# A fused two-block kernel: where the SSD's decayed inputs are made, and how row norms reach all partitions

## The chip, the cores and the metric

The kernel runs on one core of a Trainium2 chip. A core has TensorE (PE: matmuls; PEld: its weight loads), VectorE (DVE), ScalarE (ACT), GpSimd (POOL) and SyncE (SP, which here issues nearly all DMA transfers), an on-chip memory of 128 partitions (SBUF), matmul accumulators (PSUM) and DRAM. The metric is the device time of one execution in microseconds (us), lower is better, as the median of several runs.

## The reference

The input x is 512 tokens by 1024 channels, float32. The first block prepends 16 meta tokens and computes one projection of the normalised input, from which come

- an SSD (state space) branch: a causal convolution of 3072 channels; dt = softplus; per head cs = cumsum(dt * a) over a chunk; the inputs x * dt; a term inside the chunk, `y_diag = (C B^T * exp(cs_l - cs_s)) (x dt)`; a state per chunk, `states = B^T (exp(cs_end - cs) * x dt)`, carried along the chunks; then y * silu(z), **an RMS norm over each of 4 groups of 512 channels**, and a projection to 1024 channels;
- a sliding-window attention branch with meta tokens and sinks;
- gates for both, an output projection and the residual, then a convolutional feed-forward with its own RMS norm.

The second block normalises again and computes an HGRN2 recurrence and a latent attention (**RMS norms of the query and key-value latents**), gates, an output projection, the residual and a last RMS norm. An RMS norm is `y = x * rsqrt(mean(x*x) + eps)` over the channels, one factor per token.

## The kernel before

Activations lie channels on partitions and tokens along the free dimension: eight tiles of 128 channels by 528 tokens in the first block (514 where the 14 earliest tokens are no longer needed), 128 by 512 in the second. Each float32 operand of the large matmuls is split into a high and a low part, and three matmuls (L88, L89, L90) make one product. A weight tile of 128 by 1024 is loaded by SP (`wload`, L71, two buffers `wraw`), split by ACT (`whi`, L76) and by DVE (`wlo`, L77), three buffers each, and used for two halves of the tokens. PSUM tiles have tags with a number of buffers: in the first block ps_g (the projections) 3, ps_a 2, ps_t 2, ps_o 1.

Since channels are on partitions, the factor of a norm is a row of tokens that every partition needs. `SumSq` adds squares, `sums` (L169) sums them over the partitions by matmuls with a column of ones, which leaves one value per token with tokens on partitions (103 partitions by 5 columns for 514 tokens, 128 by 4 for 512). `rsqrt` computes the factor there with small DVE instructions (rq_m, rq_u, rq_y; L107 to L112, three Newton steps). `bcast_rows` then turns it back: for every column of rq_y one fp32 matmul against the identity (L129), in which rq_y is broadcast as the weight, puts the row on all 128 partitions of a PSUM tile, and ACT copies it to SBUF (L131), with a factor if wanted. `norm512` is the same for 128 by 4.

The SSD runs over four groups of eight heads, in chunks of 106 tokens. `group_tiles` makes the convolved B, C and four x tiles (xs) of the next group, `pair_a` and `pair_b` handle two heads at a time: `pair_a` transposes xs by PE (L384, a PSUM tile for chunks 0 to 3, another for chunk 4), DVE multiplies by dt into xd (L385), GpSimd multiplies xd of chunks 0 to 3 by the decay to the chunk's end into xe (L390), and xe with the transposed B gives the chunk states (L409). E, the decay inside a chunk, starts as a DMA that broadcasts one row of the cumulative sums in DRAM (csd) to all partitions (L397) and is finished by GpSimd and ACT; L440 multiplies it with xd. `pair_b` makes the gate z, adds the parts of y and splits the result into yh and yl.

After the last pair of a group, `group_end` computes the group's factor rq_y, broadcasts it into Rg (with the factor 0.5 that the gate's form needs) and returns four `branch` jobs. A branch job loads a weight tile, runs four gemms of twelve matmuls (two output tiles, two halves of the tokens) into ps_g, and DVE multiplies each by Rg into acc or bt (L477), which frees the PSUM tile. The jobs of a group are handed out among the pairs of the next group; those of the last group run beside the attention. In the second block R1 (the factor of the second block's input, used in `block_input`, L874) and the factors of the kv and q latents (`norm` in `lora_jobs`, tiles with tag lf) go through `norm512`.

No order is written out by hand beyond the program's text. A planner (`TileContext` with `schedule_with_timeline_sim=True`) simulates the program with its own costs, takes for every engine and queue the ready instruction that stands first in the text (weight loads are marked as of high priority), and fixes that order; on the chip each engine and each DMA queue works through its list strictly in order and waits on semaphores. Two instructions that share a tile's buffer wait for each other in the same way.

Of the kernel before, what the change touches and what calls it, by code (L numbers as in the profile page):

```python
# [23 lines left out]
NO = 514  # L24
# [106 lines left out]
        nc.scalar.activation(dst[:, c0 * rows:e], ps[:, :e - c0 * rows], AF.Copy, scale=fac)  # L131


class SumSq:


# [34 lines left out]
                    start=(i == 0 and c == 0), stop=(i == m and c == self.nchunk - 1))  # L171
        return ps[:r, :self.nchunk]

    def rstd(self, width, tag, ptag="t"):
        return rsqrt(self.g, self.sums(ptag), self.rows, self.nchunk, 1.0 / width, tag)


def pcol(g, name, i=0, n=1):
# [36 lines left out]
class Mixer:  # L215
# [50 lines left out]
    def steps(self, wk, dp):  # L266
        g, nc = self.g, self.nc
        wd = [t.rearrange("p a b -> p (a b)") for t in self.w0]
        slots = [tuple(t[:, k * 32:k * 32 + 32] for t in wd) for k in range(8)]
        dtf = wk.tile([32, NTP], F32, name="dtf", tag="ec", bufs=2)  # L270
        nc.gpsimd.memset(dtf[:, NT:NTP], 0.0)
        o = 0
        for n in H1:
            ps = psum(g, "a")
            gemm(g, ps[:32, :n], slots, self.u, o, n)
            nc.vector.tensor_tensor(dtf[:, o:o + n], ps[:32, :n], self.R[:32, o:o + n], ALU.mult)
            o += n
        pst = psum(g)
        for c in range(NCH):
            nc.tensor.transpose(pst[:CH, c * 32:c * 32 + 32], dtf[:, c * CH:(c + 1) * CH], g.ident[:32, :32])  # L280
        sm = lambda nm: wk.tile([128, NCH, 32], F32, name=nm, tag=nm, bufs=1)
        dt, cs, dst, dec, da = sm("dt"), sm("cs"), sm("dstt"), sm("dec"), sm("da")
        dtr, au, sz, sp = da, dst, cs, dec
        fl = lambda t: t.rearrange("p a b -> p (a b)")[:CH]
        dtb = g.par[:CH, _BP["dtb"]:_BP["dtb"] + 32].unsqueeze(1).broadcast_to([CH, NCH, 32])
        nc.vector.tensor_tensor(dtr[:CH], pst[:CH, :NCH * 32].rearrange("p (a b) -> p a b", a=NCH), dtb, ALU.add)
        nc.vector.scalar_tensor_tensor(fl(au), fl(dtr), -1.0, fl(dtr), ALU.mult, ALU.max)
        nc.scalar.activation(fl(au), fl(au), AF.Exp, scale=-1.0)

        nc.vector.tensor_scalar(fl(sp), fl(au), 1.0, 2.0, ALU.mult, ALU.add)  # L290
        nc.vector.reciprocal(fl(sp), fl(sp))
        nc.vector.tensor_tensor(fl(au), fl(au), fl(sp), ALU.mult)
        nc.vector.tensor_tensor(fl(sz), fl(au), fl(au), ALU.mult)
        nc.vector.tensor_scalar(fl(sp), fl(sz), 1.0 / 17.0, None, ALU.mult)
        for k in (15, 13, 11, 9, 7, 5, 3):
            nc.vector.scalar_tensor_tensor(fl(sp), fl(sp), 1.0 / k, fl(sz), ALU.add, ALU.mult)
        nc.vector.scalar_tensor_tensor(fl(sp), fl(sp), 1.0, fl(au), ALU.add, ALU.mult)
        nc.vector.tensor_scalar(fl(sp), fl(sp), 2.0, None, ALU.mult)
        nc.vector.scalar_tensor_tensor(fl(sp), fl(dtr), 0.0, fl(sp), ALU.max, ALU.add)
        nc.vector.memset(dt[:], 0.0)  # L300
        nc.vector.tensor_copy(dt[:CH, :NCH - 1, :], sp[:CH, :NCH - 1, :])
        nl = NT - CH * (NCH - 1)
        nc.vector.tensor_copy(dt[:nl, NCH - 1, :], sp[:nl, NCH - 1, :])
        ea = wk.tile([128, 32], F32, name="ea", tag="ea", bufs=1)
        nc.scalar.activation(ea, g.par[:, _BP["alog"]:_BP["alog"] + 32], AF.Exp)
        nc.vector.scalar_tensor_tensor(da[:CH], dt[:CH], -1.0, ea[:CH].unsqueeze(1).broadcast_to([CH, NCH, 32]), ALU.mult, ALU.mult)
        pc = psum(g)
        nc.tensor.matmul(pc[:CH, :NCH * 32], g.tri[:CH, :CH], fl(da), start=True, stop=True)
        pt = psum(g)
        nc.tensor.matmul(pt[:, :NCH * 32], g.ones[:CH, :], fl(da), start=True, stop=True)  # L310
        nc.scalar.activation(fl(cs), pc[:CH, :NCH * 32], AF.Copy)
        decf = dec.rearrange("p a b -> p (a b)")
        nc.vector.tensor_tensor(fl(dst), pt[:CH, :NCH * 32], fl(cs), ALU.subtract)
        nc.scalar.activation(fl(dst), fl(dst), AF.Exp)
        nc.scalar.activation(decf, pt[:, :NCH * 32], AF.Exp)
        cst = wk.tile([32, NTP], F32, name="cst", tag="ec", bufs=2)
        for c0, c1 in ((0, 3), (3, 5)):
            px = psum(g)
            for c in range(c0, c1):
                nc.tensor.matmul(px[:32, (c - c0) * CH:(c - c0 + 1) * CH], da[:CH, c, :], g.tri[:CH, :CH], start=True, stop=True)  # L320
            nc.scalar.activation(cst[:, c0 * CH:c1 * CH], px[:32, :(c1 - c0) * CH], AF.Copy)
        csd = dp.tile([32, NTP], F32, name="csd", tag="csd", bufs=1)
        nc.sync.dma_start(out=csd, in_=cst)
        self.dt, self.cs, self.dst, self.dec, self.csd = dt, cs, dst, dec, csd
# [48 lines left out]
    def pair_a(self, wk, gi, i):  # L373

        g, nc = self.g, self.nc
        cbm, bt, C, xs = self.grp
        dt, cs, dst, dec = self.dt, self.cs, self.dst, self.dec
        h0 = gi * 8 + 2 * i
        xd = wk.tile([128, NCH, 128], F32, name="xd", tag="xd", bufs=2)
        dtx = lambda c0, c1, t: t[:CH, c0:c1, h0:h0 + 2].unsqueeze(3).broadcast_to([CH, c1 - c0, 2, 64])  # L380
        for c0, c1 in ((0, 4), (4, 5)):
            px = psum(g)
            for c in range(c0, c1):
                nc.tensor.transpose(px[:CH, (c - c0) * 128:(c - c0 + 1) * 128], xs[i][:, c * CH:(c + 1) * CH], g.ident)  # L384
            nc.vector.tensor_tensor(  # L385
                xd[:CH, c0:c1, :].rearrange("p c (h d) -> p c h d", h=2),
                px[:CH, :(c1 - c0) * 128].rearrange("p (c h d) -> p c h d", h=2, d=64),
                dtx(c0, c1, dt), ALU.mult)
        xe = wk.tile([128, 4, 128], F32, name="xe", tag="xe", bufs=1)
        nc.gpsimd.tensor_tensor(  # L390
            xe[:CH].rearrange("p c (h d) -> p c h d", h=2),
            xd[:CH, 0:4, :].rearrange("p c (h d) -> p c h d", h=2), dtx(0, 4, dst), ALU.mult)
        Es = []
        ec = wk.tile([128, NTP], F32, name="ec", tag="ec", bufs=2)
        for k in range(2):
            E = wk.tile([128, NTP], F32, name="E", tag="E", bufs=4)
            nc.sync.dma_start(out=E, in_=self.csd[h0 + k:h0 + k + 1, :].broadcast_to([128, NTP]))  # L397
            hk = slice(k * 64, k * 64 + 64)
            nc.scalar.activation(ec[hk, CH:], E[hk, CH:], AF.Exp)
            nc.gpsimd.tensor_tensor(  # L400
                r3(E)[:CH], cs[:CH, :, h0 + k:h0 + k + 1].broadcast_to([CH, NCH, CH]), r3(E)[:CH], ALU.subtract)
            nc.scalar.activation(E[:CH, :], E[:CH, :], AF.Relu)
            nc.scalar.activation(E[:CH, :], E[:CH, :], AF.Exp, scale=-1.0)
            nc.gpsimd.tensor_tensor(E[:CH, :], E[:CH, :], cbm[:CH, :], ALU.mult)
            Es.append(E)

        px = psum(g)
        for c in range(4):
            nc.tensor.matmul(px[:, c * 128:(c + 1) * 128], bt[:CH, c, :], xe[:CH, c, :], start=True, stop=True)  # L409
        S = wk.tile([128, 4, 128], F32, name="S", tag="S", bufs=2)  # L410
        nc.scalar.activation(S[:, 0, :], px[:, 0:128], AF.Copy)
        for c in range(1, 4):
            for k in range(2):
                ks = slice(k * 64, k * 64 + 64)
                nc.vector.scalar_tensor_tensor(
                    S[:, c, ks], S[:, c - 1, ks], dec[:, c, h0 + k:h0 + k + 1],
                    px[:, c * 128 + k * 64:c * 128 + k * 64 + 64], ALU.mult, ALU.add)
        return xd, Es, ec, S, C, xs[i]
# [38 lines left out]
    def group_end(self, wk, gi):  # L457

        g = self.g
        rg = self.ssq.rstd(2048.0, "g", "o")  # L460
        Rg = self.mp.tile([128, NO], F32, name="Rg", tag="Rg", bufs=2)
        bcast_rows(g, Rg, rg, ROWS, 5, NO, 0.5, "o")
        rhs = self.rhs
        return [lambda c2=c2: self.branch(wk, gi, c2, rhs, Rg) for c2 in range(4)]

# [354 lines left out]
class Block2:  # L820
# [191 lines left out]
    def lora_jobs(self):  # L1012
# [42 lines left out]

        def norm(name):
            r = self.t("lf")
            norm512(g, self.rl[name], r)
            self.rl[name] = (self.rl[name], r)

        def gate(h):
# [138 lines left out]
    def run(self, r1, r12):  # L1200
        self.forgets()
        self.R1 = self.t("R1")
        norm512(self.g, r1, self.R1)
        self.ya = []
        jobs, kpe, norm = self.lora_jobs()
        prev = self.hgrn_a(0)
# [138 lines left out]
def two_hybrid_blocks(ctx, tc, aps):  # L1345
# [21 lines left out]
    g.ones = cp.tile([128, 128], F32, name="ones", tag="ones")  # L1367
    nc.gpsimd.memset(g.ones, 1.0)
    h1 = []
    first_mixer(g, h1)  # L1370
    ffn(g, h1)
    pctx.close()
# [155 lines left out]
```

## Time and profile before

| | |
|---|---|
| median of 3 runs | 1819.78 us (1816.46 to 1825.48) |
| the profiled execution | 1816.29 us, its span 1814.5 us |
| PE busy | 1760.9 us (97%) |
| DVE busy | 1135.3 us (63%) |
| ACT busy | 752.0 us (41%) |
| POOL busy | 321.8 us (18%) |
| DMA | 158.34 MB, mean 87 GB/s |
| mean granted TensorE clock | 0.992 |

The profile gives, for one execution, busy times by engine, groups of instructions (source line, engine, operation, tile written <- tiles read, shapes, count | busy us, mean ns of one | idle time of the engine before them, with what ended it), the chain of waits followed back from the last instruction, DMA issues with the time from issue to landing, and a timeline. An fp32 matmul leaves two records. Matmuls overlap, so the mean of one is longer than what it costs in a row of them.

### The profile page before, as it was taken

Reading aid. Unit: us, or ns where it says so; the run is one execution under the profiler, and the core shown is the slowest. Engines: PE = TensorE matmul, PEld = TensorE weight load, DVE = VectorE, ACT = ScalarE, POOL = GpSimd, SP = SyncE. Lnnn points to the kernel's source line nnn. Section 1 sums busy time; section 2 is a strip of 40 time slices with the busy share of each in tenths; the row PEclk is TensorE's granted clock in tenths of the full one; section 3 lists DMA queues with packets and bytes.
Section 4 is the critical chain, followed back from the end, with each engine's and each line's share of the span. In section 5 each row is a group of like instructions: output and inputs, shape, how many; then the busy total and the mean of one; then the engine's idle time right before and its main releaser. Section 6 shows DMA issues by size and latency. Waiting matters only on the chain.

```text
span 1814.5 us, 29816 instructions
## 1 busy us (share of the span) xinstructions
PE 1760.9 (97%) x12068; PEld 1588.9 (88%) x12068; DVE 1135.3 (63%) x2140; ACT 752.0 (41%) x1326; POOL 321.8 (18%) x300
## 2 busy tenths in 40 slices
PE   7999999999899999999999999999999899999997
PEld 7989999999898889999999888878888777788886
DVE  7897787855586645466666533576665467743453
ACT  4444444422345643343444333554342445532332
POOL 2344445523330001200000011100000121000112
PEclk9999999999999999999999999999999999999998
DMA  3323232232222132222222222222222121222222
GB/s 142 106 85 105 82 106 84 94 106 84 100 81 66 63 105 94 94 82 94 91 85 93 90 94 96 82 93 70 70 70 93 54 73 48 70 92 94 93 90 73
DMA packets 51310, 158.34 MB, mean 87 GB/s; under 512 B 5922, under 2 KB 9764, under 8 KB 51172
## 3 DMA queue, kind: packets, MB, share of 16 engines
q1 hardware_dynamic: 49252, 153.91, 25.1%
q10 hardware_dynamic: 1872, 2.39, 0.4%
q8 instruction: 95, 1.56, 0.3%
q14 instruction: 43, 0.35, 0.1%
q0 software_dynamic: 48, 0.13, 0.0%
HBM read 152.93 MB, written 2.16 MB: 85 GB/s over the span
## 4 chain that ended last, share of the span: by engine, by line
PE 84%; DVE 7%; ACT 3%; issue 2%; POOL 2%; DMA 2%; SPq 0%; DVEq 0%; POOLq 0%; ACTq 0%
PE ps_g L88 22%; PE ps_g L90 22%; PE ps_g L89 22%; PE ps_g L810 2%; PE ps_g L809 2%; PE ps_g L811 2%; DVE wlo L77 1%; DVE cv L336 1%; PE ps_o L1194 1%; DMA E<-csd 1%; PE ps_t L642 1%; PE ps_a L953 1%; POOL xe L390 1%; PE ps_a L440 1%; PE ps_t L409 1%
## 5 line engine op out<-in xcount | busy, mean ns | idle before, releaser
L76 ACT ACTIVATE whi<-wraw 128x1024 fp32r<-128x1024 f32 (+2 forms) x265 | 274.7, 1037 | 571.3 <-PE ps_g L89 348.8
L77 DVE TENSOR_TENSOR wlo<-wraw,whi 128x1024 fp32r<-128x1024 f32 (+3 forms) x259 | 335.0, 1294 | 151.7 <-ACT whi L76 151.0
L88 PE MATMUL ps_g<-uh,whi 128*128 128x264 f32 (+2 forms) x1056 | 303.7, 288 | 2.4 <-DVE z L186 1.4
L90 PE MATMUL ps_g<-uh,wlo 128*128 128x264 f32 (+2 forms) x1056 | 300.9, 285 | 0.0
L89 PE MATMUL ps_g<-ul,whi 128*128 128x264 f32 (+2 forms) x1056 | 300.7, 285 | 0.0
L88 PEld LDWEIGHTS ps_g<-uh,whi 128*128 128x128 f32 x1056 | 199.4, 189 | 4.7 <-DVE z L186 1.6
L88 PE MATMUL ps_g<-fh,whi 128*128 128x258 f32 (+1 forms) x704 | 199.9, 284 | 0.8 <-DVE fx L186 0.8
L89 PE MATMUL ps_g<-fl,whi 128*128 128x256 f32 (+1 forms) x704 | 200.3, 285 | 0.0
L90 PE MATMUL ps_g<-fh,wlo 128*128 128x256 f32 (+1 forms) x704 | 199.9, 284 | 0.0
L90 PEld LDWEIGHTS ps_g<-uh,wlo 128*128 128x128 f32 x1056 | 199.2, 189 | 0.7 <-issue 0.5
L89 PEld LDWEIGHTS ps_g<-ul,whi 128*128 128x128 f32 x1056 | 199.1, 189 | 0.3 <-issue 0.2
L88 PE MATMUL ps_g<-vh,whi 128*128 128x512 f32 x464 | 185.6, 400 | 1.8 <-DVE lf L842 1.8
L89 PE MATMUL ps_g<-vl,whi 128*128 128x512 f32 x464 | 184.6, 398 | 0.0
L90 PE MATMUL ps_g<-vh,wlo 128*128 128x512 f32 x464 | 183.9, 396 | 0.3 <-DVE wlo L77 0.3
L159 POOL TENSOR_TENSOR sq<-sq 128x514 f32<-128x514 f32 (+2 forms) x48 | 61.9, 1298 | 499.1 <-ACT sq L151 499.1
L88 PEld LDWEIGHTS ps_g<-fh,whi 128*128 128x128 f32 x704 | 134.0, 190 | 1.0 <-DVE fx L186 1.0
L89 PEld LDWEIGHTS ps_g<-fl,whi 128*128 128x128 f32 x704 | 134.5, 191 | 0.0
L90 PEld LDWEIGHTS ps_g<-fh,wlo 128*128 128x128 f32 x704 | 134.5, 191 | 0.0
L88 PEld LDWEIGHTS ps_g<-vh,whi 128*128 128x128 f32 x464 | 87.4, 188 | 20.4 <-ACT whi L76 2.2
L90 PEld LDWEIGHTS ps_g<-vh,wlo 128*128 128x128 f32 x464 | 87.2, 188 | 19.6 <-DVE wlo L77 0.8
L89 PEld LDWEIGHTS ps_g<-vl,whi 128*128 128x128 f32 x464 | 87.3, 188 | 18.4
L88 PE MATMUL ps_g<-yh,whi 128*128 128x258 f32 (+1 forms) x256 | 75.8, 296 | 1.7 <-DVE bt L477 1.1
(434 smaller groups left out, 3834.8 us busy)
## 6 DMA issues: line engine op xcount, KB each, us to landing
wraw<-in_w_in SPq DMA_DIRECT2D x128, 512.0 KB, 3.2
wraw<-in_w_ffn_in SPq DMA_DIRECT2D x44, 512.0 KB, 3.2
E<-csd SPq DMA_DIRECT2D x32, 265.0 KB, 4.1
wraw<-in_w_ssd SPq DMA_DIRECT2D x16, 512.0 KB, 3.2
wraw<-in_w_out SPq DMA_DIRECT2D x16, 512.0 KB, 3.3
wraw<-in_w_ffn_out SPq DMA_DIRECT2D x16, 512.0 KB, 3.2
wraw<-in_w_pab SPq DMA_DIRECT2D x16, 512.0 KB, 3.3
wraw<-in_w_att SPq DMA_DIRECT2D x8, 512.0 KB, 3.2
```

Of the source, the lines that this page charges most:

```text
L76: nc.scalar.activation(hf[:, :n], raw[:, :n], AF.Copy)
L77: (eng or nc.vector).tensor_tensor(lf[:, :n], raw[:, :n], hf[:, :n].bitcast(F32), ALU.subtract)
L88: nc.tensor.matmul(ps, wh, a, start=(i == 0), stop=False)
L89: nc.tensor.matmul(ps, wh, b, start=False, stop=False)
L90: nc.tensor.matmul(ps, wl, a, start=False, stop=(i == last))
L159: self.g.nc.gpsimd.tensor_tensor(a[:, :self.ntok], a[:, :self.ntok], sq[:, :self.ntok], ALU.add)
L336: nc.vector.scalar_tensor_tensor(cv, xr[:, j:j + NT], w(j), cv, ALU.mult, ALU.add)
L390: nc.gpsimd.tensor_tensor(xe[:CH].rearrange("p c (h d) -> p c h d", h=2), xd[:CH, 0:4, :].rearrange("p c (h d) -> p c h d", h=2), dtx(0, 4 ...
L409: nc.tensor.matmul(px[:, c * 128:(c + 1) * 128], bt[:CH, c, :], xe[:CH, c, :], start=True, stop=True)
L809: nc.tensor.matmul(ps, wh, uh, start=(k == 0), stop=False)
L810: nc.tensor.matmul(ps, wh, ul, start=False, stop=False)
L811: nc.tensor.matmul(ps, wl, uh, start=False, stop=(k == NFF - 1))
```

## The change

1. **Decayed inputs.** In `steps`, the decay factors `dst` are multiplied by dt once (one DVE instruction). In `pair_a`, xe is then made by DVE from the transposed x in PSUM and `dst`, right after the first part of xd; GpSimd's instruction on xd goes away.
2. **Norms by DRAM.** A new function, `bcast_dram`, writes the factor from SBUF into a row in DRAM, in token order, and reads that row back into all 128 partitions, two transfers on SP's queue, the second dependent on the first. It takes the place of the broadcast by matmuls and ACT for the four group norms (103 by 5), for R1 and for the kv and q latents (128 by 4): seven calls. The factor 0.5 of the group norm moves into rsqrt (`fac`). The other norms stay as they were: the first block's input, the feed-forward's, r12 of the second block, the last one.

```diff
+def bcast_dram(g, pool, dst, y, rows, nchunk, ntok):
+
+    nc = g.nc
+    d = pool.tile([1, nchunk * rows], F32, name="rowd", tag="rowd", bufs=2)
+    nc.sync.dma_start(out=d.rearrange("o (c r) -> (o r) c", r=rows), in_=y)
+    nc.sync.dma_start(out=dst, in_=d[:, :ntok].broadcast_to([128, ntok]))
@@ class SumSq
-    def rstd(self, width, tag, ptag="t"):
-        return rsqrt(self.g, self.sums(ptag), self.rows, self.nchunk, 1.0 / width, tag)
+    def rstd(self, width, tag, ptag="t", fac=1.0):
+        f = fac ** -2.0
+        return rsqrt(self.g, self.sums(ptag), self.rows, self.nchunk, f / width, tag, EPS * f)
@@ steps
         nc.scalar.activation(fl(dst), fl(dst), AF.Exp)
+        nc.vector.tensor_tensor(fl(dst), fl(dst), fl(dt), ALU.mult)
@@ pair_a
                 dtx(c0, c1, dt), ALU.mult)
-        xe = wk.tile([128, 4, 128], F32, name="xe", tag="xe", bufs=1)
-        nc.gpsimd.tensor_tensor(
-            xe[:CH].rearrange("p c (h d) -> p c h d", h=2),
-            xd[:CH, 0:4, :].rearrange("p c (h d) -> p c h d", h=2), dtx(0, 4, dst), ALU.mult)
+            if c0 == 0:
+                xe = wk.tile([128, 4, 128], F32, name="xe", tag="xe", bufs=1)
+                nc.vector.tensor_tensor(
+                    xe[:CH].rearrange("p c (h d) -> p c h d", h=2),
+                    px[:CH].rearrange("p (c h d) -> p c h d", h=2, d=64), dtx(0, 4, dst), ALU.mult)
@@ group_end
-        rg = self.ssq.rstd(2048.0, "g", "o")
+        rg = self.ssq.rstd(2048.0, "g", "o", 0.5)
         Rg = self.mp.tile([128, NO], F32, name="Rg", tag="Rg", bufs=2)
-        bcast_rows(g, Rg, rg, ROWS, 5, NO, 0.5, "o")
+        bcast_dram(g, g.dp, Rg, rg, ROWS, 5, NO)
@@ lora_jobs, norm
-            norm512(g, self.rl[name], r)
+            bcast_dram(g, g.dp, r, self.rl[name], 128, 4, NX)
@@ Block2.run
-        norm512(self.g, r1, self.R1)
+        bcast_dram(self.g, self.g.dp, self.R1, r1, 128, 4, NX)
@@ two_hybrid_blocks
+    g.dp = ctx.enter_context(tc.tile_pool(name="rows", bufs=1, space=bass.MemoryType.DRAM))
```

## The prediction

> **What bounds the kernel now.** I read the page first, its shares and its chain of waits.
>
> ```profile
> span 1814.5 us, 29816 instructions
> PE 1760.9 (97%) x12068; PEld 1588.9 (88%) x12068; DVE 1135.3 (63%) x2140; ACT 752.0 (41%) x1326; POOL 321.8 (18%) x300
> PE 84%; DVE 7%; ACT 3%; issue 2%; POOL 2%; DMA 2%; SPq 0%; DVEq 0%; POOLq 0%; ACTq 0%
> ```
>
> PE is busy 97% of the span and carries 84% of the chain, so the kernel is a stream of matmuls. An edit gains what it takes out of that stream or out of the few places where PE stands, and loses wherever it makes PE stand. All of this execution is 1816.29 us, 1.8 us more than its span, and lies 3.5 us under the median of the runs, 1819.78. I add to the execution's time; the offset to the median is a fifth of a percent.
>
> The diff works mostly in the SSD groups, which in the timeline fill 80 to 500 us. The busy times of that stretch:
>
> ```profile
> core 0: us, PE busy (x) PEld busy (x) DVE busy (x) ACT busy (x) POOL busy (x), PEclk, DMA share, GB/s
> 80.00:500.00 420.00, 404.10 (x3503) 395.05 (x3501) 305.92 (x539) 173.18 (x264) 187.29 (x177) 1.00 0.28 93
> ```
>
> PE stands still for 16 us of 420 there; DVE is busy 73% and has room. Now the groups of instructions that the diff removes or relieves (busy, mean, and the engine's idle time before them):
>
> ```profile
> L129 PE MATMUL ps_t<-mats,rq_y 128*128 128x128 f32 (+3 forms) x54 | 7.2, 275 | 0.9 <-DVE rq_y L112 0.9
> L129 PE MATMUL ps_o<-mats,rq_y 103*128 103x103 f32 (+1 forms) x40 | 6.1, 283 | 5.3 <-DVE rq_y L112 4.7 <-ACT Rg L131 0.6
> L409 PE MATMUL ps_t<-xe,bt 106*128 106x128 f32 x128 | 17.8, 282 | 6.4 <-POOL xe L390 6.0 <-POOL xr L330 0.3
> L390 POOL TENSOR_TENSOR xe<-xd,dstt 106x512 f32<-106x512 f32 x16 | 25.1, 1571 | 24.8 <-DVE xd L385 24.8
> ```
>
> Of PE's 16 us, 6.0 go to waits for GpSimd's xe and 5.3 to waits around the broadcasts of the groups' norms. The stage's stalls are thus exactly where the change works.
>
> **The change part by part: xe.** Before, xe follows two steps: DVE writes xd, then GpSimd takes 1571 ns. After, DVE makes it from the same PSUM tile. Its nearest price is the first part of xd, same shape, same source:
>
> ```profile
> L385 DVE TENSOR_TENSOR xd<-ps_t,dt 106x512 f32<-106x512 f32 x16 | 10.9, 680 | 0.0
> ```
>
> xe comes 0.68 us after xd instead of 1.57 or more, so I credit PE with the whole wait of 6.0 us. DVE gets 16 times 0.68 = 10.9 us more, which its idle 114 us of the stretch cover; if none of it were covered this part would lose 4.9 us. The one extra multiplication of the decay factors by dt, a small DVE instruction (160 elements a partition), is put at nothing; its cover is the same DVE idle time.
>
> **Three norms of the second block** (R1, and those of kv and q). Each loses four fp32 matmuls, eight of the 54 records of the first L129 row; 24 of 54 by 7.2 us is 3.2 us off PE. Each gains two transfers on SP's queue. Their rows are complete early: R1's first reader and the attention's weights come later, and I put the transfers at nothing; if the queue holds back the weights and rope copies behind the q norm, a transfer of some 3 to 4 us could show once.
>
> **The norms of the four groups** decide the case. Before: rsqrt on DVE (rq_y), five matmuls into ps_o, two evictions by ACT (Rg), and the DVE products that free the ps_g tiles of the first branch gemms. After: rq_y, a write into DRAM (time w, from the issue to landing), a wait of SP for it, a read back to 128 partitions, the same products. Group 0 in the timeline, first PE, then DVE:
>
> ```profile
> 164.24 1.13 PE L440 MATMUL ps_a<-E,xd 106*64 106x106 f32 x20
> 167.04 1.11 PE L129 MATMUL ps_o<-mats,rq_y 103*128 103x103 f32 x8 [1.67 <-DVE rq_y L112]
> 171.21 0.39 PE L88 MATMUL ps_g<-yh,whi 128*128 128x256 f32 x1
> 165.86 1.03 DVE L112 SCALAR_TENSOR_TENSOR rq_y<-rq_u,rq_y 103x5 f32<-103x5 f32 x1
> 169.16 0.75 DVE L477 TENSOR_TENSOR acc<-ps_g,Rg 128x258 f32<-128x258 f32 x2
> ```
>
> Three quarters of the branch's first unit have already run by 164.2 and hold all three ps_g tiles, so every later projection waits for Rg. The fourth quarter resumes at 171.21. The read back looks like the reads of E, which broadcast one DRAM row of nearly the same length; the write has the store of csd as its nearest row, 32 rows with few, long pieces:
>
> ```profile
> E<-csd SPq DMA_DIRECT2D x32, 265.0 KB, 4.1
> csd<-cst SPq DMA_DIRECT2D x1, 66.2 KB, 2.6
> ```
>
> So the quarter resumes at 166.89 (end of rq_y) + w + 4.1 + 0.4 (the product) = 171.4 + w: a loss of 0.2 + w, with the matmuls' saving already in it. The other groups:
>
> ```profile
> 268.51 0.16 DVE L112 SCALAR_TENSOR_TENSOR rq_y<-rq_u,rq_y 103x5 f32<-103x5 f32 x1
> 273.12 0.36 PE L88 MATMUL ps_g<-yh,whi 128*128 128x256 f32 x1
> 365.48 0.17 DVE L112 SCALAR_TENSOR_TENSOR rq_y<-rq_u,rq_y 103x5 f32<-103x5 f32 x1
> 378.61 0.42 DVE L477 TENSOR_TENSOR bt<-ps_g,Rg 128x258 f32<-128x258 f32 x1
> 381.54 0.37 PE L88 MATMUL ps_g<-yh,whi 128*128 128x256 f32 x1
> 498.48 0.17 DVE L112 SCALAR_TENSOR_TENSOR rq_y<-rq_u,rq_y 103x5 f32<-103x5 f32 x1
> 500.97 0.45 PE L88 MATMUL ps_g<-yh,whi 128*128 128x256 f32 x1
> 360.00:372.00 12.00, 1.40 (x10) 1.29 (x10) 1.00 0.25 87
> ```
>
> Group 1 resumes at 268.67 + w + 4.5 against 273.12: loss 0.1 + w. Group 3: 498.65 + w + 4.5 against 500.97: loss 2.2 + w. Group 2 runs other projections first: Rg is there at 365.65 + w + 4.1, is read at 378.61, and the fourth quarter comes only at 381.54, so w is hidden up to 11.4 us and PE saves 1.4 us (last row: the L129 matmuls' busy time in that window). Together 1.1 + 3w, and beyond 11.4 us another w - 11.4.
>
> What SP holds meanwhile: while it waits for w, the weights and E loads behind it stay unissued.
>
> ```profile
> SPq L71 <- DVE wlo L77: 1192.6, 211, 15.6
> ```
>
> SP already stands 5.7 us on average for a free weight buffer, so the loads run ahead of PE; and during w PE stands for Rg anyway. I add nothing for it.
>
> **What w is.** In each of the 103 partitions five neighbouring values go to DRAM addresses 412 bytes apart, so the row is 515 pieces of 4 bytes. No row shows such a store. From below it is 2.6 us, as if pieces cost nothing or were spread over 16 engines (32 each). From above come the smallest payloads of the trace: a window with one load of 128 pieces of 512 bytes, and one at the end with stores of 1 KB:
>
> ```profile
> DMA  0000010222147265687765644531111100000000
> DMA packets 144, 0.07 MB, mean 82 GB/s; under 512 B 16, under 2 KB 144, under 8 KB 144
> q1 hardware_dynamic: 144, 0.07, 28.4%
> ```
>
> ```profile
> DMA packets 1152, 1.05 MB, mean 300 GB/s; under 512 B 128, under 2 KB 1152, under 8 KB 1152
> q1 hardware_dynamic: 576, 0.52, 43.2%
> q10 hardware_dynamic: 576, 0.52, 42.6%
> ```
>
> The first window is 0.8 us: 28.4% of 16 engines is 3.6 us, 28 ns for each of 128; but the eight pieces of an engine take some 0.5 us (the digits, 0.02 us each), 64 ns apart. The second is 3.5 us: 85.8% of 16 engines over 1024 pieces, 47 ns for 1 KB. A line through 28 and 47 ns leaves 9 ns for a piece of almost nothing. I assume the 515 pieces run one behind the other on one engine (103 has no divisor by which the rows could be dealt out evenly), at 18 ns, the middle between 9 and 28: w = 2.6 + 9.5 = 12.1 us. Ends: 2.6 us, and 2.6 + 515 x 64 ns = 35.6 us.
>
> The Trainium skill speaks to this choice in "DMA: Bandwidth & Descriptors", section "Why a DMA increments its semaphore by 16 and not by 1": a transfer uses the largest number of engines up to 16 that divides the outermost sizes, and 127 rows fall on one engine. By that rule 103 rows use one and the three 128-row norms sixteen; no run here shows it yet. Were the 515 pieces spread instead, the sum would end near the lower bound below.
>
> **The sum.** Groups 1.1 + 36.3 + 0.7 = 38.1; xe -6.0; three norms -3.2: +28.9. 1816.3 + 28.9 is 1845 us, slower by 1.4%. DVE wholly uncovered would add 10.9, the q norm 4.
>
> **Rivals.** *The short write*: w between 2.6 and 7.2 us (9 ns a piece). The sum is 3w - 8.1: -0.3 to +13.5, so 1816 to 1830. For it speaks that stores of 1 KB at the end run without gaps. *The long write*: at 64 ns a piece, w = 35.6: groups 1.1 + 106.8 + 24.2, less 9.2, gives 1939. For it: a 4-byte store is further from a long one than anything in the trace, and the 512-byte pieces did stand 64 ns apart. *The other side*: the planner, which orders every engine by its own estimate of when things are ready, sees the longer way of Rg and puts the branch's first gemms behind other projections in all groups, as they stand in group 2. Then w is hidden up to some 11 us, and PE loses 6.1 + 3.2 us of matmuls, 5.3 of waits around them and 6.0 for xe: 20.6 us, 1796. It decides wherever 12 us of other projections precede the branch. Against it: in groups 0, 1 and 3 the gemms need only the split rows and the weights, not Rg, and nothing in the order before shows that Rg's lateness held them back. *Not what it says*: xe waits as long for DVE as it did for GpSimd, because DVE's queue is ordered otherwise; then 6.0 us are missing, 1851.
>
> **How the numbers follow.** A difference under 0.5%, 9 us, cannot be told from no change in these runs. The forecast (serial pieces of 9 to 28 ns, w to 17 us, 1830 to 1865) gets 0.42, with the missing xe gain 0.03; the short write 0.23, nearly all within 0.5%; the long one 0.17; the hidden one 0.15. Faster 0.15, same 0.22, slower 0.63. The likeliest's own range is 1830 to 1865. The range asked for runs from 1800 to 1905: it leaves out half of the hidden case and half of the long one.
>
> **What would show it.** In the issues of transfers a row for rowd with its time to landing (w, 12 us by me, and 3 to 4 us for the norms of 128 rows); PE standing before an L88 matmul of the branch in groups 0, 1 and 3, ended by a DVE product that waits for the DMA into Rg, w longer than now; no such wait in group 2; no wait for xe before the L409 matmuls, and DVE instructions of some 0.68 us for xe. I am wrong if w is under 5 us, if the branch gemms come behind other projections, or if PE stands for weights instead.

## The result, and the profile after

The changed kernel takes 1869.79 us as the median of 5 runs (1868.17 to 1870.42), beside 1819.78 us (1816.46 to 1825.66) for the kernel before in the same comparison: a ratio of 1.0276, 95% interval 1.0258 to 1.0293. It is slower by 50 us, where 29 were forecast; 1869.8 lies 5 us above the likeliest case's own range of 1830 to 1865, and within the whole range of 1800 to 1905. Its profiled execution took 1868.29 us.

The page of the changed kernel, its span and its engines:

```profile
span 1866.5 us, 29730 instructions
PE 1764.2 (95%) x12004; PEld 1590.6 (85%) x12004; DVE 1136.1 (61%) x2157; ACT 747.6 (40%) x1314; POOL 290.9 (16%) x284
```

PE stands still for 1866.5 - 1764.2 = 102.3 us, against 53.6 us before: 48.7 of the 52 us by which the span grew. The other 3.3 us are PE busy for longer, and that is odd, for the edit took 3.2 + 6.1 = 9.3 us of matmuls away. So the matmuls that stayed took some 12.6 us more than before. Both parts are found below.

The group of the branch's first matmuls (instruction and shape, count | busy, mean of one | PE's idle time just before them and what ended it), first of the kernel before, then of the changed one:

```profile
L88 PE MATMUL ps_g<-yh,whi 128*128 128x258 f32 (+1 forms) x256 | 75.8, 296 | 1.7 <-DVE bt L477 1.1 <-DVE xr L186 0.4
```

```profile
L88 PE MATMUL ps_g<-yh,whi 128*128 128x258 f32 (+1 forms) x256 | 77.6, 303 | 43.8 <-DVE bt L488 31.3
```

Idle time before this one group went from 1.7 to 43.8 us. Group 0 in the timeline (start, duration), SP's queue, then DVE, then PE:

```profile
163.09 0.30 SPq L138 DMA_DIRECT2D rowd<-rq_y  x1
173.65 0.34 SPq L139 DMA_DIRECT2D Rg<-rowd  x1
```

```profile
162.91 0.15 DVE L112 SCALAR_TENSOR_TENSOR rq_y<-rq_u,rq_y 103x5 f32<-103x5 f32 x1
178.80 1.09 DVE L488 TENSOR_TENSOR acc<-ps_g,Rg 128x258 f32<-128x258 f32 x3 [12.15 <-DMA Rg<-rowd]
```

```profile
179.29 0.58 PE L88 MATMUL ps_g<-yh,whi 128*128 128x256 f32 x1 [12.07 <-DVE acc L488]
179.67 0.41 PE L89 MATMUL ps_g<-yl,whi 128*128 128x256 f32 x1
182.83 0.28 PE L89 MATMUL ps_g<-ul,whi 128*128 128x258 f32 x1
```

The store is issued at 163.09 and the read back, which waits for it, at 173.65: w is 10.6 us. The read back is in use 5.15 us later, and PE, which had no free PSUM tile, stood for 12.07 us. The last two rows show something else: matmuls of the same kind last 0.41 us just after the stall and 0.28 us from 182.83 on.

The other groups, end of rq_y on DVE and PE's next branch matmul:

```profile
276.30 0.16 DVE L112 SCALAR_TENSOR_TENSOR rq_y<-rq_u,rq_y 103x5 f32<-103x5 f32 x1
526.68 0.17 DVE L112 SCALAR_TENSOR_TENSOR rq_y<-rq_u,rq_y 103x5 f32<-103x5 f32 x1
```

```profile
292.94 0.58 PE L88 MATMUL ps_g<-yh,whi 128*128 128x256 f32 x1 [10.20 <-DVE bt L488]
543.02 0.58 PE L88 MATMUL ps_g<-yh,whi 128*128 128x256 f32 x1 [13.63 <-DVE bt L488]
```

Group 2 ought to have hidden its row behind other projections. Its SP queue, DVE and PE:

```profile
387.98 0.24 SPq L138 DMA_DIRECT2D rowd<-rq_y  x1
398.62 0.32 SPq L139 DMA_DIRECT2D Rg<-rowd  x1
399.04 0.86 SPq L71 DMA_DIRECT2D wraw<-in_w_in  x2
```

```profile
406.75 1.22 DVE L77 TENSOR_TENSOR wlo<-wraw,whi 128x1024 fp32r<-128x1024 f32 x1 [9.57 <-ACT whi L76]
407.89 1.08 DVE L488 TENSOR_TENSOR bt<-ps_g,Rg 128x258 f32<-128x258 f32 x3
```

```profile
408.36 0.58 PE L88 MATMUL ps_g<-yh,whi 128*128 128x256 f32 x1 [6.34 <-DVE bt L488]
```

Here the product with Rg has no wait of its own. It stands in DVE's queue behind a weight split, the split waits for its weights, and the weights were issued only at 399.04, after SP had been held for 10.6 us. PE stands for 6.34 us on a chain that starts in SP's queue.

In the second block R1 and the q norm cost stalls too, by two different ways; SP first, then DVE at R1, then PE:

```profile
1193.36 0.39 SPq L138 DMA_DIRECT2D rowd<-rq_y  x1
1203.49 0.34 SPq L139 DMA_DIRECT2D R<-rowd  x1
1468.79 0.38 SPq L138 DMA_DIRECT2D rowd<-rq_y  x1
1476.88 0.33 SPq L139 DMA_DIRECT2D lf<-rowd  x1
1477.31 2.51 SPq L1088 DMA_DIRECT2D th<-lf  x4
```

```profile
1207.44 5.39 DVE L885 SCALAR_TENSOR_TENSOR h<-h,par,R 128x512 f32<-128x512 f32 x8 [10.46 <-DMA R<-rowd]
```

```profile
1216.29 0.49 PE L88 MATMUL ps_g<-vh,whi 128*128 128x512 f32 x1 [3.87 <-ACT whi L76]
1486.41 1.25 PE L1017 MATMUL ps_t<-mats,o 128*128 128x128 f32 x4 [7.22 <-ACT o L1013]
```

These stores have 128 rows, and still w is 10.1 and 8.1 us. At R1 the row itself is late: DVE waits 10.46 us for it, ACT works on what DVE makes, the next weight split (whi) stands behind that in ACT's queue, and PE waits for the split. At q the four rope copies (th) are late: SP issues them only at 1477.31, after it was held; DVE's product with them waits 8.53 us, and the factor rq_y of another norm, for which ACT's L1013 waits, stands behind that product. The kv row, whose read back is issued 33 us after its store with five weight loads in between, costs no stall of over 1 us.

### The profile page after: what moved, and what is told of

Its sections match the earlier page's. It is cut to its first block, busy times and chain, and to the rows that moved or that the text cites. A ratio compares the mean times of both kernels' runs of the same rounds, so it can differ in the third digit from the quotient of the medians.

```text
span 1866.5 us, 29730 instructions
## 1 busy us (share of the span) xinstructions
PE 1764.2 (95%) x12004; PEld 1590.6 (85%) x12004; DVE 1136.1 (61%) x2157; ACT 747.6 (40%) x1314; POOL 290.9 (16%) x284
## 3 DMA queue, kind: packets, MB, share of 16 engines
q8 instruction: 94, 1.54, 0.4%
## 4 chain that ended last, share of the span: by engine, by line
PE 63%; DVE 4%; DMA 2%; ACT 1%; issue 1%; SPq 0%; DVEq 0%; ACTq 0%
PE ps_g L88 16%; PE ps_g L90 16%; PE ps_g L89 16%; PE ps_g L821 2%; PE ps_g L820 2%; PE ps_g L822 2%; DMA rowd<-rq_y 2%; PE ps_o L1205 1%; PE ps_a L964 1%; PE ps_t L653 1%; PE ps_o L664 1%; DVE wlo L77 0%; PE ps_a L615 0%; PE ps_o L663 0%; PE ps_o L644 0%
## 5 line engine op out<-in xcount | busy, mean ns | idle before, releaser
L88 PE MATMUL ps_g<-yh,whi 128*128 128x258 f32 (+1 forms) x256 | 77.6, 303 | 43.8 <-DVE bt L488 31.3
```

The source lines that it names most:

```text
L88: nc.tensor.matmul(ps, wh, a, start=(i == 0), stop=False)
```

## The experiments

The edits are shown against the kernel before, unless another is named. `bcast_dram` and `fac` are those of the change.

**One part at a time.** Three kernels each hold one part of the change.

*xe alone.*

```diff
+        nc.vector.tensor_tensor(fl(dst), fl(dst), fl(dt), ALU.mult)
-        xe = ... nc.gpsimd.tensor_tensor(xe, xd[:CH, 0:4, :], dtx(0, 4, dst), ALU.mult)
+            if c0 == 0:
+                xe = ... nc.vector.tensor_tensor(xe, px[:CH], dtx(0, 4, dst), ALU.mult)
```

> The kernel before with part 1 alone: xe by VectorE from PSUM, all norms by matmuls. Theory (the two parts add up, and xe is nearly worthless): the changed kernel still shows 5.9 us of TensorE waits for xe, as the one before did (6.0), so 0 to 3 us faster, 1817 to 1820 us. My prediction's own step: 6.0 us faster, 1814. Rival (VectorE, 10.9 us busier, is what slows the changed kernel): 5 us slower or more.

Measured: 1813.29 us against 1819.24 before, ratio 0.9966 (0.9953 to 0.998): 6.0 us faster, as the prediction's own step had it; the theory that xe is nearly worthless is out. The group that uses xe, in this kernel and then in the changed one:

```profile
L411 PE MATMUL ps_t<-xe,bt 106*128 106x128 f32 x128 | 17.4, 279 | 4.1 <-DVE xe L392 3.9
```

```profile
L420 PE MATMUL ps_t<-xe,bt 106*128 106x128 f32 x128 | 18.0, 284 | 5.9 <-DVE xe L401 5.9
```

The size is the forecast's, but PE still waits 3.9 us for xe, now for DVE's, where it waited 6.0. The rows put some 2 us of the gain at this wait. PE's idle time fell by 3.4 us in all in the profiled execution, which was 4.3 us faster than that of the kernel before; which other waits the rest of the 6.0 came from is not settled.

*The four groups' norms alone.*

```diff
-        bcast_rows(g, Rg, rg, ROWS, 5, NO, 0.5, "o")
+        bcast_dram(g, g.dp, Rg, rg, ROWS, 5, NO)
```

> The kernel before with the four group norms by DRAM alone. Theory: the stalls before the branch gemms in the changed kernel (12.1, 10.2, 6.3, and 3.6 + 13.6 us) less what the broadcasts cost before (about 5 us of matmuls, 5.3 us of waits) plus some 2 us each for matmuls at half clock right after a stall: 38 us slower, 1853 to 1863 us. Rival (the losses come from both parts together, a busier VectorE making the row late): under 25 us slower.

Measured: 1865.94 us, ratio 1.0255 (1.023 to 1.028), 46.7 us slower, 3 us above the expected range. SP's wait between the two transfers (total, times, longest):

```profile
SPq L139 <- DMA rowd<-rq_y: 42.1, 4, 10.7
```

Four waits of 10.5 us each: nearly the whole loss of the change comes with these four rows. PE's stalls in front of the branch matmuls are 13.15, 10.29, 5.59 and 14.06 us, in the order of the groups.

*R1 and the two latents alone.*

```diff
-            norm512(g, self.rl[name], r)
+            bcast_dram(g, g.dp, r, self.rl[name], 128, 4, NX)
-        norm512(self.g, r1, self.R1)
+        bcast_dram(self.g, self.g.dp, self.R1, r1, 128, 4, NX)
```

> The kernel before with R1 and the kv and q norms by DRAM alone. Theory (a store of a row holds SP for about 10 us whatever its shape, and weights and rope copies behind it come late): 3.9 + 2.6 us at R1 and 7.2 + 2.1 us less the 4.3 us that stood there before at the q norm, less 2.7 us of matmuls: 8 to 12 us slower, 1828 to 1832. My prediction's own step: 3.2 us faster, 1817. Rival (these stalls follow from the order that the first block's change brought): no slower than 1822.

Measured: 1831.63 us, ratio 1.0067 (1.0043 to 1.0091): 12.4 us slower, where the prediction had a gain of 3.2. The stalls stand where the changed kernel has them (3.87 and 2.07 us after R1; 7.55 and, right behind it, 2.08 us at q, where the kernel before has one of 4.09). The time lies in the range expected for late transfers behind SP (1828 to 1832); at R1, though, it is again the row itself for which DVE waits, 10.45 us. The three parts sum to -6.0 + 46.7 + 12.4 = 53 us; the whole change measured 50.

**Is it the short pieces?** The changed kernel, but rq_y is first turned by one matmul, copied by ACT into the first rows of the destination tile, and stored as 5 pieces of 412 B (4 of 512 B in the second block). Against the changed kernel:

```diff
-    nc.sync.dma_start(out=d.rearrange("o (c r) -> (o r) c", r=rows), in_=y)
+    ps = psum(g, "o" if rows == ROWS else "t")
+    nc.tensor.transpose(ps[:nchunk, :rows], y, g.ident[:rows, :rows])
+    nc.scalar.activation(dst[:nchunk, :rows], ps[:nchunk, :rows], AF.Copy)
+    nc.sync.dma_start(out=d.rearrange("o (c r) -> (o c) r", r=rows), in_=dst[:nchunk, :rows])
```

> The changed kernel, but the factors are first transposed by one matmul and copied by ScalarE, so that the row goes to DRAM in 5 pieces of 412 bytes (or 4 of 512) in place of 515 (512) of 4 bytes; everything else stays. Theory (the 4-byte pieces are what the store's time is made of): the store takes 2 to 3 us in place of 10.5, the read back can start 7 us earlier in groups 0, 1 and 3, the late weights of group 2, R1 and the q norm go away: 1826 to 1840 us. Rival (a dependent round trip through DRAM costs 10 us whatever the pieces): the store still takes over 8 us, 1865 or more.

Measured: 1815.02 us, ratio to the kernel before 0.9977 (0.9965 to 0.9988), 55 us less than the changed kernel and better than every expectation. SP's queue at group 0:

```profile
163.71 0.32 SPq L141 DMA_DIRECT2D rowd<-Rg  x1
165.73 0.32 SPq L142 DMA_DIRECT2D Rg<-rowd  x1
```

w is 2.0 us where it was 10.6, for the same bytes at the same place. The long stalls are gone. The way through DRAM is thus not what costs, the form of the store is.

**What in the store costs.** Ten extra stores in the feed-forward, each followed by a read back of 4 bytes; the kernel is the one before otherwise, and the stores' data is used by nothing. Each store ran once, in one execution.

```diff
+    src = wk.tile([128, 8], F32, ...); nc.gpsimd.tensor_copy(src, x[:, :8])
+    d = g.dp.tile([1, rows * n * max(gap, 1)], F32, ...)
+    nc.sync.dma_start(out=out, in_=src[:rows, :n])   # out: view of d, pieces gap * 4 bytes apart
+    nc.sync.dma_start(out=back, in_=d[:, :1])
```

> The kernel before with ten extra stores to DRAM on SyncE's queue during the feed-forward, each followed by a read back of 4 bytes; nothing else is changed, and the time is not the question. Stores, in rows of the source by pieces per row: 103x5, 96x5, 128x4, 128x2, 128x1 of 4-byte pieces laid side by side; 128x4 with the pieces 64 B and 512 B apart; 128x4 as 128 pieces of 16 B; 103x5 with the pieces 64 B apart; 103x5 as 103 pieces of 20 B. Theory A (each piece has its price, some 16 ns, however many engines send it): from the issue of the store to the issue of the read back 103x5, 96x5 and 128x4 take 9 to 11 us each, 128x2 some 6, 128x1 some 4, the spaced ones as long as the packed ones, 16-byte and 20-byte pieces some 4. Theory B (the price is that of small pieces that fall side by side in the same stretch of DRAM): as A for the packed ones, but the pieces 64 B or 512 B apart land in some 3 to 5 us. Theory C (the number of engines that share the transfer decides, and the 128-row stores were late only because of what else was under way): 103x5 10 us, 96x5 and 128x4 some 3 us.

SP's timeline of this kernel for six of the ten, in the order 103x5, 128x4 and 128x1 side by side, 128x4 with the pieces 64 B apart, 128 pieces of 16 B, and 103x5 with the pieces 64 B apart; a store, then its read back:

```profile
804.74 0.26 SPq L782 DMA_DIRECT2D pd<-src  x1
815.28 0.24 SPq L784 DMA_DIRECT2D bk<-pd  x1
...
851.10 0.39 SPq L782 DMA_DIRECT2D pd<-src  x1
860.80 0.25 SPq L784 DMA_DIRECT2D bk<-pd  x1
...
897.44 0.33 SPq L782 DMA_DIRECT2D pd<-src  x1
904.90 0.24 SPq L784 DMA_DIRECT2D bk<-pd  x1
920.62 0.38 SPq L782 DMA_DIRECT2D pd<-src  x1
922.65 0.24 SPq L784 DMA_DIRECT2D bk<-pd  x1
...
966.96 0.33 SPq L782 DMA_DIRECT2D pd<-src  x1
968.38 0.24 SPq L784 DMA_DIRECT2D bk<-pd  x1
990.14 0.26 SPq L782 DMA_DIRECT2D pd<-src  x1
997.38 0.24 SPq L784 DMA_DIRECT2D bk<-pd  x1
```

All ten, from the issue of the store to the issue of the read back:

| source rows x pieces a row | layout in DRAM | us |
|---|---|---|
| 103 x 5 of 4 B | side by side | 10.5 |
| 96 x 5 of 4 B | side by side | 7.2 |
| 128 x 4 of 4 B | side by side | 9.7 |
| 128 x 2 of 4 B | side by side | 7.8 |
| 128 x 1 of 4 B | side by side | 7.5 |
| 128 x 4 of 4 B | 64 B apart | 2.0 |
| 128 x 4 of 4 B | 512 B apart | 1.8 |
| 128 x 1 of 16 B | side by side | 1.4 |
| 103 x 5 of 4 B | 64 B apart | 7.2 |
| 103 x 1 of 20 B | side by side | 2.4 |

No single theory holds. With 128 rows, 128 pieces side by side take nearly as long as 512, and 512 pieces set 64 B apart take 2.0 us: neighbourhood in DRAM is what costs there, as theory B has it, and a price per piece (A) is out. With 103 rows the distance helps only from 10.5 to 7.2 us, and the number of pieces does count: 103 of 20 B take 2.4. That would fit a serial stream, (7.2 - 2.4) / (515 - 103) = 12 ns for each further piece. Theory C, that the number of engines decides, is out for stores side by side: 96 x 5 and 128 x 4 took 7.2 and 9.7 us where it had some 3. With the pieces 64 B apart its difference does show, 7.2 us from 103 rows and 2.0 from 128.

That a store can have left long before it counts as landed can be seen in the changed kernel. Its windows of 11 us from the store's issue on, group 0 and then R1: the mean busy share of the 16 DMA engines in 40 slices of 0.275 us, and the packets:

```profile
DMA  9521100111110112002011110110200000000000
DMA packets 574, 0.18 MB, mean 16 GB/s; under 512 B 532, under 2 KB 532, under 8 KB 573
```

```profile
DMA  9910260000000000000000000000000000000000
DMA packets 609, 0.27 MB, mean 24 GB/s; under 512 B 544, under 2 KB 544, under 8 KB 609
```

Group 0's pieces trickle for some 8 us at about a tenth of the engines' capacity and less; R1's 512 are all sent within 2 us, and yet its row counts as landed only 10 us after the issue. By the Trainium skill's rule that was cited in the prediction ("DMA: Bandwidth & Descriptors", section "Why a DMA increments its semaphore by 16 and not by 1") 103 rows go out on one engine and 128 on sixteen. These digits agree with it; but for stores side by side it made no difference to the landing. Why neighbours of 4 bytes take so long, and neighbours of 16 bytes don't, no run here tells: the neighbours of a 4-byte piece also come from other rows of the source, and the two were not tried apart.

**Is it SP's held queue?** The three norms of the second block by DRAM, with both transfers on GpSimd's queue (the edit of `bcast_dram` is shown against the change's):

```diff
-    nc.sync.dma_start(out=d.rearrange("o (c r) -> (o r) c", r=rows), in_=y)
-    nc.sync.dma_start(out=dst, in_=d[:, :ntok].broadcast_to([128, ntok]))
+    nc.gpsimd.dma_start(out=d.rearrange("o (c r) -> (o r) c", r=rows), in_=y)
+    nc.gpsimd.dma_start(out=dst, in_=d[:, :ntok].broadcast_to([128, ntok]))
```

> The kernel before with the three norms of the second block (R1, kv, q) by DRAM as in the changed kernel, but both transfers of each issued on GpSimd's queue, so that SyncE's queue of weights and rope tables is held by none of them. If SyncE's held queue makes the loss of 12 us that these three had on SyncE's queue: 1817 to 1823 us, and the gaps of TensorE of 3.9, 7.6 and 2.1 us at these places are gone or under 2 us each. If the row itself comes too late: still 1828 to 1834 us, with the gaps before the same products. If GpSimd's own work is held instead (it stands in the same way while it waits for the store): its late products make gaps of their own, 1825 to 1835 us.

Measured: 1827.9 us, ratio 1.0052 (1.0036 to 1.0067); 9.4 us of the 12.4 remain, and the stalls (4.95 and 1.54 us after R1, 9.25 at q) stand at the same places. Freeing SP's queue gave back 3 us. At R1 the way is the one above, the late row:

```profile
DVE h L882 <- DMA R<-rowd: 12.1, 1, 12.1
```

GpSimd's own hold is not what costs: at R1 it has nothing to do for 27 us after the read back, and at q its next product waits another 4.1 us for the rope copies after the hold has ended. The transfers issued from 1428 to 1450 us, around the q norm, show what else goes wrong (KB each, median time from issue to landing); below them the same rope copies in the kernel before:

```profile
wraw<-in_w_uq SPq DMA_DIRECT2D x1, 512.0 KB, 9.5
th<-lf SPq DMA_DIRECT2D x4, 64.0 KB, 8.9
...
rowd<-rq_y POOLq DMA_DIRECT2D x1, 2.0 KB, 9.7
```

```profile
th<-lf SPq DMA_DIRECT2D x4, 64.0 KB, 2.9
```

Freed of the wait, SP issues its weights and rope copies at once, and they land 9 us later instead of 3, beside a store of 2 KB. The data of the first three rope copies had passed by 1433.1, 3 us after their issue (0.20 MB on SP's queue between 1429.5 and 1434); it is their landing that waited. DVE's product with the copies waits 7.8 us for them, where it waited 8.9 with the copies held behind SP. So the transfers beside such a store land late here, though another queue issued it. R1's loss goes through the late row and q's through the late copies; how the 9.4 us divide between them is not measured.

**Is there a version that wins?** Two kernels with xe by DVE and long pieces (the store of the fourth experiment), one for the groups alone, one for the second block alone; the other norms stay on matmuls.

```diff
-        bcast_rows(g, Rg, rg, ROWS, 5, NO, 0.5, "o")
+        bcast_dram(g, g.dp, Rg, rg, ROWS, 5, NO)      # turned, 5 pieces of 412 B
```

> The changed kernel with the second block's three norms back on matmuls, and the groups' rows turned by one matmul and stored as 5 pieces of 412 B. xe by VectorE alone was worth 6 us. If the short stores of the four groups are hidden in full: 1810 to 1814 us. If each of groups 0, 1 and 3 still costs the 1 to 2 us by which 2 us of store and 4 to 5 us of read back outlast the matmuls that they replace: 1814 to 1819 us.

And, with R1 likewise:

```diff
-            norm512(g, self.rl[name], r)
+            bcast_dram(g, g.dp, r, self.rl[name], 128, 4, NX)      # turned, 4 pieces of 512 B
```

> The changed kernel with the four groups' norms back on matmuls, and the second block's three rows turned by one matmul and stored as 4 pieces of 512 B. If the three are hidden once the store is short, TensorE saves the some 1 us of matmuls of each: 1809 to 1813 us. If SyncE's queue, held for 2 us instead of 8 to 10, still makes weights late: 1814 to 1818 us.

Measured: groups 1811.12 us, ratio 0.9959 (0.9947 to 0.9972); second block 1815.85 us, ratio 0.9981 (0.9972 to 0.999). Beside xe alone (0.9966) the groups' short store neither gains nor loses anything that these runs can tell; the second block's seems to give 2 to 3 us back even so, though the two intervals overlap. So the best of these kernels are 6 to 7.5 us faster than the one before, and xe alone gives as much as these runs can tell; the way through DRAM, with its store put right, comes out even with the matmuls at best.

Last, the groups without the turning, with xe by DVE and the second block's norms on matmuls (the second edit is of the change's `bcast_dram`): a group's sums are taken for columns 5r to 5r+4 on row r, so that each row of rq_y leaves as one piece of 20 B.

```diff
-                    ps[:r, c:c + 1], t[:, c * r:(c + 1) * r], self.g.ones[:, 0:1],
+                    ps[:r, c:c + 1], t[:, c::self.nchunk] if by_row else t[:, c * r:(c + 1) * r], self.g.ones[:, 0:1],
-    nc.sync.dma_start(out=d.rearrange("o (c r) -> (o r) c", r=rows), in_=y)
+    nc.sync.dma_start(out=d.rearrange("o (r c) -> (o r) c", c=nchunk), in_=y)
```

> xe by VectorE and the four groups' norms by DRAM, as in the changed kernel; the second block's three norms stay on matmuls. The sums of a group are taken for columns 5r to 5r+4 on row r instead of r, r+103 and so on, so that each of the 103 rows leaves as one piece of 20 B, with no matmul and no ScalarE copy for turning it. Store to read back 2 to 3 us (the stores tried apart: 2.4 us for 103 pieces of 20 B). If the pieces are what cost: 1808 to 1814 us, TensorE's gaps before the groups' branch products under 2 us each. If a store from 103 rows by one engine stays long beside the kernel's own transfers (8 us or more): 1835 to 1855 us. If reading the squares with a stride of five slows the 20 matmuls of sums or what stands behind them: 1815 to 1825 us.

Measured: 1824.45 us, ratio 1.0034 (1.002 to 1.0047), a miss of the expectation for short pieces: the store took 2.3 us at group 0 as expected, and yet the kernel is some 11 us slower than xe alone. The time lies in the range of the third reading (slower sums), but the sums are only part of it: their 40 records are busy 7.4 us (310 ns each) where they took 4.0 (225 ns) with xe alone. The read back, in this kernel and then in the one with turned rows:

```profile
Rg<-rowd SPq DMA_DIRECT2D x4, 257.0 KB, 4.2
```

```profile
Rg<-rowd SPq DMA_DIRECT2D x4, 257.0 KB, 3.3
```

It lands 0.9 us later, and PE stands 3.03, 2.32 and 5.19 us before the branch matmuls of groups 0, 1 and 3, where the kernel with turned rows has less than 1.1 us at each. Why the same read back takes longer here was not tried. The profiled execution, the fastest of the six, is 8.0 us slower than that of xe alone. Its PE stands 58.0 us instead of 50.2, which is all of it; PE's busy time is the same, 1760.0 us, though 6.1 us of broadcasts are gone, and of what fills their place 3.4 us are the sums.

## Why the prediction was right and wrong

**The direction and the mechanism held.** The groups decide, PE stands before the branch's matmuls in groups 0, 1 and 3 because the PSUM tiles wait for Rg, and w sets how long. From the end of rq_y to PE's next branch matmul I had 12.1 + 4.1 + 0.4 = 16.6 us in group 0; the rows show 179.29 - 163.06 = 16.2, and 16.5 and 16.2 in groups 1 and 3. Two errors cancel in that: w is 10.6 to 11.1 us and not 12.1, the read back 5.1 and not 4.1. The short write (w up to 7.2) and the long one (35.6) are both out. So is the planner's other order: the branch gemms were not moved behind other projections.

**The price of a piece was near for a reason that holds only in part, and so partly by luck.** I took 515 pieces in a row on one engine at 18 ns. Set 64 B apart they do stream so, at 12 ns, to 7.2 us; side by side the store is 10.5 us, and side by side it is as slow on sixteen engines. With that the second half of the reasoning fails: that the pieces, were they spread over 16 engines, would come near the lower bound.

**The step that failed most is "I put the transfers at nothing", for the three norms of the second block.** The forecast was -3.2 us and the run of that part gives +12.4: 15.6 us missed, the most of any step (the groups missed 8.6; the parts miss 24 together, the whole 21). Two premises stood behind it. "Their rows are complete early" fails at R1, where the reader on DVE waited 10.46 us for the row, by the trace of the changed kernel. And "a transfer of some 3 to 4 us could show once" saw rightly that the rope copies behind q's store would be held, but had the store with 128 rows at under half of its measured 8.1 us.

**"What SP holds meanwhile: I add nothing for it" failed in group 2.** Those 6.3 us are late weights behind SP's wait. I had the row of that group hidden up to 11.4 us of w; at 10.6 us its product indeed does not wait for the row, but it stood behind the weight split in DVE's queue.

**What no step had: the stalls slow the work behind them.** After group 0's stall PE's matmuls start every 0.21 us until 182.83 and every 0.12 us from there: 3.5 us at about half speed, some 1.6 us lost. Behind the stalls of groups 1, 2 and 3 it is 5.8, 3.1 and some 5 us. These windows of the kernel before and the changed one (PE busy, PEld, DVE, ACT, POOL; then the granted clock) show it as a clock:

```profile
165.00:195.00 30.00, 28.33 (x248) 27.61 (x244) 21.85 (x39) 12.32 (x19) 10.62 (x11) 1.00 0.31 107
```

```profile
165.00:195.00 30.00, 17.71 (x143) 17.18 (x142) 11.58 (x26) 8.18 (x14) 6.74 (x7) 0.77 0.33 81
```

A mean clock of 0.77 over 30 us amounts to half the clock for 13.8 us, most of the stall and the 3.5 us behind it. Of the 12.6 us by which the remaining matmuls got longer, the runs of the parts show 6.8 for the groups (PE busy 1761.6 us, where 1760.9 less 6.1 us of broadcasts would be 1754.8) and 5.0 for the second block (1762.7 against 1757.7). The Trainium skill has this rule in "TensorE: Matmul & The Clock Gate", section "Part 1: The HAM clock gate": an idle PE is gated to half its clock and gets it back after some 3.4 us of work. The trace agrees in groups 0 and 2 (3.5 and 3.1 us); in groups 1 and 3 it took longer.

**The groups' sum**, 38.1 us forecast against 46.7 in the run of that part: 6.8 us for the clock and about 5 for group 2, less 1 for the three others, make 38.1 + 10.8 = 48.9; the remaining 2 us are open.

**xe.** The credit of 6.0 us is what its run gave (3.6 to 8.6 us by the interval), but partly by luck: the wait that was to vanish shrank by 2 us only. The expected sign, no wait for xe before its matmuls, is wrong: PE waits 5.9 us for DVE's xe in the changed kernel. Of the rival that xe waits as long for DVE, the wait is there but the missing gain is not.

## What to carry to other kernels

Price a small DMA by the pieces it makes and by where they land: 2 KB stored as 4-byte neighbours took 8 to 11 us, as pieces of 412 or 512 B 1.2 to 2.3 us, and one matmul that turns the tile first pays for itself many times over. Even then compare with what stands there: here the broadcast by matmuls was no worse. Before a dependent pair of transfers goes on the queue that feeds the weights, list what is behind it; here a wait of 10 us reached PE through weights that had nothing to do with it. And add to each stall of PE of several us the slow start behind it, 3 to 6 us at half speed here.

## What the hardware showed that was not expected

Sixteen engines did not help a store of 4-byte pieces side by side: 128 such pieces, 512 bytes in all, took 7.5 us, and 512 pieces 64 B apart took 2.0. Beside such a store other transfers landed late, though another queue issued it: at the q norm 512 KB of weights took 9.5 us (median 3.2 in the changed kernel), and a weight load issued at 1157.84 beside R1's store on GpSimd's queue still had half of its bytes to move after 1166.
